# The weight sums of a Strassen–Winograd feed-forward layer in pair order on GpSimd: low products last, stores behind later loads

## The chip, the cores and the metric

The kernel runs on one core of a Trainium2 chip. The metric is the device time of one launch in microseconds; before the change the median of three runs is 1889.56 us (1884.88 to 1890.27).

Five engines work side by side, each with a queue of its own that is served in order: PE (TensorE, matmuls; its loading of weights is listed apart as PEld), DVE (VectorE), ACT (ScalarE), POOL (GpSimd) and SP (SyncE, which issues nearly all DMAs). An instruction that waits holds back everything behind it in its own queue.

## The reference

Two sequences, a prompt of 256 and a sample of 512 positions, go through two layers of a model of width 1024. The first layer mixes positions by an mLSTM in both directions, the second by attention in a window. Behind each mixer stands the feed-forward part, on which the change works:

```python
def conv_ffn(h, w_up, conv_w, conv_b, w_down):          # D_FF = 2816
    u = h @ w_up                                         # 1024 -> 5632
    u = conv_general_dilated(u, conv_w, width 3, one channel each) + conv_b
    g, val = u[..., :D_FF], u[..., D_FF:]
    return (jax.nn.silu(g) * val) @ w_down               # 2816 -> 1024

for l in range(2):
    ...
    x = x + g1 * mixer(rmsnorm(x, norm_g[l, 0]) * (1 + sc1) + sh1)
    h = rmsnorm(x, norm_g[l, 1]) * (1 + sc2) + sh2
    x = x + g2 * conv_ffn(h, ...)
return rmsnorm(x, final_g)
```

All is float32.

## The kernel before

**Precision.** A float32 matrix product is made of three products of rounded halves: high by high, high by low and low by high. `split` makes the halves of a weight tile of 128 x 1024 (`raw`, loaded by SP): ACT casts the high half (`whi`, line 262), then DVE subtracts it from the tile (`wlo`, line 263).

**Up-projection.** The 768 columns of both sequences are halved into two times 384 (H). The 2816 channels are cut into 11 parts (p = 0 to 10), and each part has two units of weights (i = 0 for the gate, 1 for the value). `pair` multiplies one unit by Strassen and Winograd's scheme: seven products of quarters in place of eight. `quarters` is one product: 4 slices of the inner dimension by 3 products of halves, 12 matmuls of 128x128 by 384. A pair has 84 matmuls, a part 168. The products are programmed as B11, T1 (weights `s1h`, `s1l`), T2, B21, T3, B22, T4. I name a pair by part and unit: (3,1) is the second pair of part 3.

The operands of the activations are ready in advance (`yh`, `yl`, `zh`, `zl`). Those of the weights are made on POOL, four instructions a pair on the two loaded tiles `ra` and `rb`: line 1204 (q2 += q3, wants only `rb`), 1207 (into `ra`, wants the split `wa` of `ra` to be done), 1208, and 1216 (into `rb`, wants `s1l` made). From the sums ACT and DVE split `s1`, `wc` and `wb`. `wa` serves B11 and B21, `wc` T2 and B22, `wb` T3 and T4. The tile pool holds five raw tiles, so the loads run about two pairs ahead. ACT also copies sums of PSUM between banks in a pair (lines 1219, 1226, 1232, 1243) and evicts results (1184); DVE adds two of them (1245, 1246).

**Convolution and product.** `conv` makes the three taps (ACT 1489, DVE 1491 and 1492), `silu` the gate (ACT 1499). Then parts 0, 1 and 10 are multiplied by `product` and their down-projection is made part by part. The eight parts 2 to 9 (`g is None`, SOLO = 2, NBLK = 8) go another way: `operands` multiplies gate and value on POOL (line 1510, four instructions a part), `combine` makes Strassen's combinations on DVE (lines 1515 to 1518), and the result is stored to DRAM (`yd`, 1344 KB, line 1520). After the last pair, `blocked` makes the down-projection of the eight parts in seven steps of 96 matmuls. It fetches each step's `yd` (line 1285), loads weights (1289), makes sums on POOL (1300) and stores some of them (`sd`, 1302). The activations `xt` are saved to DRAM in between (`xf`, line 388) and added again at the end.

**Order.** PE, ACT, DVE and POOL get their orders from a scheduler that walks the program with estimated times; `issue_after` binds an instruction behind another. Steps are hung on a pair by dictionaries, `later[p, i]` and `held`, and run in the middle of that pair, behind the fourth copy (`behind`, in `pair`). In before, `operands` of part p hangs on pair (p+1,1), `combine` and the store on (p+2,0). Numbers below are in the order p, i.

## Time and profile before

| | |
|---|---|
| median of 3 runs | 1889.56 us (1884.88 to 1890.27) |
| profiled execution | 1893.23 us, of which the span of instructions 1891.4 us |
| busy: PE, DVE, ACT, POOL | 95%, 72%, 50%, 29% of the span |
| mean granted clock of PE | 0.978 |
| read from and written to HBM | 231.09 MB and 40.38 MB, 144 GB/s over the span |

The pairs of parts 5 to 9 follow each other in a steady pattern: in the first layer from 708.6 to 869.7 us of the span, in the second from about 1524 to 1685 us.

Times in rows are microseconds from the span's start. A row of the timeline has start, duration, engine, line, operation, out<-in and count, then in brackets how long the engine had been idle before and what released it. A row of the waits has the total, the number and the longest. A row of the windows has stretch, length, busy time with instruction counts for each engine, granted clock, share of the DMA engines and GB/s.

### The profile page before, as it was taken

To read this page: it belongs to the slowest core of one execution; us is meant where nothing else is said; L and a number is where in the kernel's file an instruction comes from. 1 tells how busy PE (TensorE), PEld (TensorE's weight loads), DVE (VectorE), ACT (ScalarE), POOL (GpSimd) and SP (SyncE) were. 2 spreads that over 40 slices of the span, in tenths; PEclk is the share of its full clock that TensorE was granted. 3 is DMA by queue.
4 is the path that set the end of the run, shared out by engine and by line. 5 is a ranking of instruction groups with operands and counts; after the bars stand their busy time and mean duration, and the time that the engine had idled before them with its cause. 6 is when DMAs were issued, how large, how long until landed. Compare 5 with 4: busy or idle time off the path is not lost.

```text
span 1891.4 us, 29178 instructions
## 1 busy us (share of the span) xinstructions
PE 1791.8 (95%) x11098; PEld 1674.2 (89%) x11098; DVE 1365.6 (72%) x2093; ACT 952.3 (50%) x1935; POOL 553.0 (29%) x450
## 2 busy tenths in 40 slices
PE   7999999999999989998899999999999999998997
PEld 4988888989998989998899999989989899997997
DVE  4765677885798676776868857767997677777685
ACT  3444434443565455554544556665554555555453
POOL 2101001030124345656220214320242555644201
PEclk9999999999999999999899999999999999998998
DMA  8343566455212433234797321133123232356872
GB/s 328 113 155 125 169 203 228 152 169 189 69 58 66 133 105 117 96 134 169 240 315 239 102 89 45 55 117 111 55 69 123 97 125 97 126 177 195 312 251 67
DMA packets 111735, 273.36 MB, mean 145 GB/s; under 512 B 8599, under 2 KB 51095, under 8 KB 109804
## 3 DMA queue, kind: packets, MB, share of 16 engines
q1 hardware_dynamic: 109292, 263.12, 41.6%
q0 software_dynamic: 2304, 8.39, 1.1%
q8 instruction: 87, 1.43, 0.3%
q14 instruction: 52, 0.43, 0.1%
HBM read 231.09 MB, written 40.38 MB: 144 GB/s over the span
## 4 chain that ended last, share of the span: by engine, by line
PE 55%; DVE 13%; POOL 12%; DMA 9%; issue 7%; ACT 3%; SPq 0%; POOLq 0%; DVEq 0%; ACTq 0%
PE ps L256 24%; PE pa L256 10%; DMA raw<-in_w_dram 7%; POOL slab L1510 4%; DVE wlo L263 4%; PE ps L1174 3%; PE ps L1171 3%; PE ps L1172 3%; POOL raw L1208 2%; PE ps L1343 2%; PE ps L1342 2%; PE ps L1344 2%; POOL raw L1207 2%; POOL raw L1204 2%; PE pa L1010 1%
## 5 line engine op out<-in xcount | busy, mean ns | idle before, releaser
L263 DVE TENSOR_TENSOR wlo<-raw,whi 128x1024 fp32r<-128x1024 f32 x261 | 339.4, 1303 | 103.3 <-ACT whi L262 102.5
L262 ACT CAST whi<-raw 128x1024 fp32r<-128x1024 f32 x261 | 272.8, 1048 | 240.8 <-POOL raw L1208 49.9
L1171 PE MATMUL ps<-zh,whi 128*128 128x384 f32 x504 | 175.6, 348 | 22.3 <-ACT whi L262 13.6
L1174 PE MATMUL ps<-zh,wlo 128*128 128x384 f32 x504 | 175.9, 349 | 21.2 <-DVE wlo L263 21.2
L256 PE MATMUL ps<-zh,whi 128*128 128x256 f32 (+1 forms) x560 | 189.0, 339 | 2.3 <-ACT whi L262 1.7
L256 PE MATMUL ps<-zh,wlo 128*128 128x256 f32 (+1 forms) x560 | 184.5, 331 | 1.5 <-DVE wlo L263 1.5
L256 PE MATMUL ps<-zl,whi 128*128 128x256 f32 (+1 forms) x560 | 185.2, 333 | 0.0
L1172 PE MATMUL ps<-zl,whi 128*128 128x384 f32 x504 | 173.8, 345 | 0.8 <-DVE zl L1128 0.8
L1204 POOL TENSOR_TENSOR raw<-raw 128x512 f32<-128x512 f32 x40 | 64.9, 1623 | 270.2 <-DMA raw<-in_w_dram 246.9
L256 PE MATMUL ps<-slab,whi 128*128 128x384 f32 x512 | 132.3, 340 | 0.9 <-DVE slab L263 0.5
L1491 DVE SCALAR_TENSOR_TENSOR slab<-slab,cstt,slab 128x771 f32<-128x771 f32 x88 | 105.2, 1197 | 36.9 <-ACT slab L1489 36.8
L1171 PEld LDWEIGHTS ps<-zh,whi 128*128 128x128 f32 x504 | 97.6, 194 | 30.2 <-ACT whi L262 14.9
L508 DVE SCALAR_TENSOR_TENSOR ada<-raw,silc,ada 128x1024 f32<-128x1024 f32 x84 | 112.1, 1372 | 14.9 <-DMA raw<-in_adaln_w_dram 14.9
L1174 PEld LDWEIGHTS ps<-zh,wlo 128*128 128x128 f32 x504 | 97.8, 194 | 28.2 <-DVE wlo L263 26.6
L256 PEld LDWEIGHTS ps<-zh,whi 128*128 128x128 f32 x560 | 107.7, 193 | 15.8 <-issue 4.4
L1489 ACT ACTIVATE slab<-slab,cstt 128x772 f32<-128x772 f32 x88 | 91.2, 1036 | 55.8 <-DVE slab L1245 55.3
L256 PEld LDWEIGHTS ps<-zl,whi 128*128 128x128 f32 x560 | 107.5, 193 | 12.0 <-issue 3.4
L256 PEld LDWEIGHTS ps<-zh,wlo 128*128 128x128 f32 x560 | 107.5, 192 | 11.7 <-DVE wlo L263 2.4
L1492 DVE SCALAR_TENSOR_TENSOR slab<-slab,cstt,slab 128x771 f32<-128x771 f32 x88 | 113.8, 1293 | 0.3
L1174 PE MATMUL ps<-yh,wlo 128*128 128x384 f32 x304 | 104.6, 344 | 6.3 <-DVE wlo L263 6.3
L1171 PE MATMUL ps<-yh,whi 128*128 128x384 f32 x304 | 103.7, 341 | 0.0
L1172 PE MATMUL ps<-yl,whi 128*128 128x384 f32 x304 | 103.5, 341 | 0.0
(315 smaller groups left out, 5017.8 us busy)
## 6 DMA issues: line engine op xcount, KB each, us to landing
raw<-in_w_dram SPq DMA_DIRECT2D x248, 512.0 KB, 4.2
raw<-in_adaln_w_dram SPq DMA_DIRECT2D x84, 512.0 KB, 4.7
yd<-slab SPq DMA_DIRECT2D x14, 1344.0 KB, 4.6
slab<-yd SPq DMA_DIRECT2D x14, 768.0 KB, 7.7
sd<-raw POOLq DMA_DIRECT2D x16, 512.0 KB, 5.6
raw<-sd SPq DMA_DIRECT2D x16, 512.0 KB, 5.6
slab<-in_x_dram SPq DMA_DIRECT2D x12, 512.0 KB, 6.5
slab<-in_adaln_w_dram SPq DMA_DIRECT2D x12, 512.0 KB, 10.3
```

The lines of the kernel that those rows point to most:

```text
L256: self.nc.tensor.matmul(out, lhsT, rhs, start=start, stop=stop)
L262: nc.scalar.copy(hi, src)
L263: return nc.vector.tensor_tensor(lo, src, hi.bitcast(F32), ALU.subtract)
L508: stt(acc[:, s], row, w, acc[:, s], ALU.mult, ALU.add)
L1171: mm(o, wh[:, k], hi[k], start=start and k == 0, stop=False, skip_group_check=True)
L1172: mm(o, wh[:, k], lo[k], start=False, stop=False, skip_group_check=True)
L1174: mm(o, wl[:, k], hi[k], start=False, stop=k == 3, skip_group_check=True)
L1204: tt(q[2], q[2], q[3], ALU.add)
L1489: nc.scalar.activation(y, u, AF.Identity, bias=cb, scale=w(1))
L1491: stt(y[:, 1:], u[:, :-1], w(0), y[:, 1:], ALU.mult, ALU.add)
L1492: stt(y[:, :-1], u[:, 1:], w(2), y[:, :-1], ALU.mult, ALU.add)
L1510: nc.gpsimd.tensor_tensor(row[:, p0:p1], yrow[:, 2 + j, b], yrow[:, j, b], ALU.mult)
```

## The change

Line numbers of the kernel after the change are one to three lower in `pair` (1203, 1206, 1207, 1215 for the sums; 1231 for the copy 1232; 1299 and 1301 for 1300 and 1302).

- The first sum of a pair is bound behind the last sum of the pair before it or, where a part's products stand in between, behind these (`summed`).
- `quarters` makes the four low products (`wl` by high) behind the eight others in every product, on one line, 1176.
- The products (line 1510) are put between two pairs: behind the sums of pair (p+1,1), and ahead of the first sum of the next. The combining (now lines 1517 to 1520) comes behind the add into `r1` of that pair (`added`).
- The store of a part (line 1523) comes behind the loads of pair (p+2,1) on SP, and the save of `xf` behind those of pair (4,0).
- The second stream's `yd` is fetched behind the loads of the first step of `blocked`, not ahead of the last pairs, and one stop of `blocked` is dropped.

```diff
@@ quarters
-            if not low:
-                mm(o, wl[:, k], hi[k], start=False, stop=k == 3, skip_group_check=True)
         if low:
             low()
-            for k in range(4):
-                mm(o, wl[:, k], hi[k], start=False, stop=k == 3, skip_group_check=True)
+        for k in range(4):
+            mm(o, wl[:, k], hi[k], start=False, stop=k == 3, skip_group_check=True)
@@ raw / pair
-        self.nc.sync.dma_start(t, src)
+        self.loaded = self.nc.sync.dma_start(t, src)
...
-        tt(q[2], q[2], q[3], ALU.add)
+        with self.tc.issue_after(self.summed.ins) if self.summed else nullcontext():
+            tt(q[2], q[2], q[3], ALU.add)
...
-        tt(q[2], q[3], q[0], ALU.subtract)
+        self.summed = tt(q[2], q[3], q[0], ALU.subtract)
...
-        nc.vector.tensor_tensor(r1[:, col(H) :], b, p5, ALU.add)
+        self.added = nc.vector.tensor_tensor(r1[:, col(H) :], b, p5, ALU.add)
@@ blocked
         fetch(0, (0, 1))
-        fetch(1, (0, 1))
         yield
         fetch(0, (2,))
-        fetch(1, (2,))
-        yield
+        fetch(1)
@@ ffn
+        def store(s, k):
+            nc.sync.dma_start(yd[k // 2 - 1][k % 2] if k > 3 else yd[0][k], s)
+
+        def gather(yrow, k):
+            with self.tc.issue_after(self.summed.ins):
+                s = operands(yrow, k)          # its last product becomes self.summed
+            with self.tc.issue_after(self.added.ins):
+                combine(s)
+            if k == NBLK - 1:
+                self.final = s
+            else:
+                later[SOLO + k + 2, 1] = lambda: store(s, k)
+
+        def put_by():
+            for rng in RANGES:
+                self.save_x(xt, xf, rng)
...
-                        self.pair(pool, u0 + 3 * p + i, bank, rows, p == 1, lambda: [f() for f in then])
+                        self.pair(pool, u0 + 3 * p + i, bank, rows, p == 1, held.pop() if held else None)
+                    if (p, i) in moves:
+                        gather(*moves.pop((p, i)))
+                    if (p, i) in later:
+                        with self.tc.issue_after(self.loaded.ins):
+                            later.pop((p, i))()
...
-                    if p == NPART - 1:
-                        next(tail)
             if g is None:
-                later[p + 1, 1] = lambda: operands(yrow, p - SOLO)
+                moves[p + 1, 1] = yrow, p - SOLO
...
             if p == SOLO:
-                for rng in RANGES:
-                    self.save_x(xt, xf, rng)
+                later[p + 2, 0] = put_by
```

POOL in the steady parts. The tiles 7520 and 7522 before, 7519 and 7521 after, are those of the pair (7,1); 7654 and 7656, then 7658 and 7660, those of (8,0). Before:

```order
L1204 TENSOR_TENSOR raw_7785<-raw_7785 128x512
L1207 TENSOR_TENSOR raw_7522<-raw_7520,raw_7522 128x512
L1208 TENSOR_TENSOR raw_7522<-raw_7522 128x512
L1216 TENSOR_TENSOR raw_7520<-raw_7520,raw_7522 128x512
L1510 TENSOR_TENSOR slab_7586<-slab_7123 128x512
L1510 TENSOR_TENSOR slab_7586<-slab_7123 128x256
L1510 TENSOR_TENSOR slab_7586<-slab_7123 128x512
L1510 TENSOR_TENSOR slab_7586<-slab_7123 128x256
L1204 TENSOR_TENSOR raw_7919<-raw_7919 128x512
L1207 TENSOR_TENSOR raw_7656<-raw_7654,raw_7656 128x512
L1208 TENSOR_TENSOR raw_7656<-raw_7656 128x512
L1216 TENSOR_TENSOR raw_7654<-raw_7654,raw_7656 128x512
```

After:

```order
L1203 TENSOR_TENSOR raw_7519<-raw_7519 128x512
L1206 TENSOR_TENSOR raw_7521<-raw_7519,raw_7521 128x512
L1207 TENSOR_TENSOR raw_7521<-raw_7521 128x512
L1215 TENSOR_TENSOR raw_7519<-raw_7519,raw_7521 128x512
L1510 TENSOR_TENSOR slab_7641<-slab_7127 128x512
L1510 TENSOR_TENSOR slab_7641<-slab_7127 128x256
L1510 TENSOR_TENSOR slab_7641<-slab_7127 128x512
L1510 TENSOR_TENSOR slab_7641<-slab_7127 128x256
L1203 TENSOR_TENSOR raw_7658<-raw_7658 128x512
L1206 TENSOR_TENSOR raw_7660<-raw_7658,raw_7660 128x512
L1207 TENSOR_TENSOR raw_7660<-raw_7660 128x512
L1215 TENSOR_TENSOR raw_7658<-raw_7658,raw_7660 128x512
```

Before, the first sum in a group of four is that of a pair two further on (7785 beside 7520, 7919 beside 7654); after, all four are of one pair, and the products stand between the last sum of one pair and the first of the next.

POOL at the end of the pairs, around the products of part 9; the tiles 8326 and 8328 before, 8320 and 8322 after, are those of the pair (10,1), and 8473 to 8493 are weights of the block phase. Before:

```order
L1300 TENSOR_TENSOR raw_8473<-raw_8473,raw_8475 128x1024
L1302 DMA sd_8183<-raw_8473 128x1024
L1300 TENSOR_TENSOR raw_8491<-raw_8491,raw_8493 128x1024
L1207 TENSOR_TENSOR raw_8328<-raw_8326,raw_8328 128x512
L1302 DMA sd_8183<-raw_8491 128x1024
L1510 TENSOR_TENSOR slab_8392<-slab_7918 128x512
L1510 TENSOR_TENSOR slab_8392<-slab_7918 128x256
L1510 TENSOR_TENSOR slab_8392<-slab_7918 128x512
L1510 TENSOR_TENSOR slab_8392<-slab_7918 128x256
L1208 TENSOR_TENSOR raw_8328<-raw_8328 128x512
L1216 TENSOR_TENSOR raw_8326<-raw_8326,raw_8328 128x512
```

After:

```order
L1203 TENSOR_TENSOR raw_8320<-raw_8320 128x512
L1299 TENSOR_TENSOR raw_8473<-raw_8473,raw_8475 128x1024
L1301 DMA sd_8187<-raw_8473 128x1024
L1206 TENSOR_TENSOR raw_8322<-raw_8320,raw_8322 128x512
L1299 TENSOR_TENSOR raw_8491<-raw_8491,raw_8493 128x1024
L1207 TENSOR_TENSOR raw_8322<-raw_8322 128x512
L1215 TENSOR_TENSOR raw_8320<-raw_8320,raw_8322 128x512
L1510 TENSOR_TENSOR slab_8442<-slab_7922 128x512
L1510 TENSOR_TENSOR slab_8442<-slab_7922 128x256
L1510 TENSOR_TENSOR slab_8442<-slab_7922 128x512
L1510 TENSOR_TENSOR slab_8442<-slab_7922 128x256
L1301 DMA sd_8187<-raw_8491 128x1024
```

The products and the issue of a store have gone from between the second and the third sum of the pair; the second sum of the block phase stands ahead of the third in both.

PE in one product of a pair, as the difference (`whi` and `wlo` are the two halves of its weights; the rows with `pa` behind it are another stage's matmuls):

```order
 L1171 MATMUL ps_4533<-yh,whi_5163 128x384
 L1172 MATMUL ps_4533<-yl,whi_5163 128x384
-L1174 MATMUL ps_4533<-yh,wlo_5164 128x384
 L1171 MATMUL ps_4533<-yh,whi_5163 128x384
 L1172 MATMUL ps_4533<-yl,whi_5163 128x384
-L1174 MATMUL ps_4533<-yh,wlo_5164 128x384
 L1171 MATMUL ps_4533<-yh,whi_5163 128x384
 L1172 MATMUL ps_4533<-yl,whi_5163 128x384
-L1174 MATMUL ps_4533<-yh,wlo_5164 128x384
 L1171 MATMUL ps_4533<-yh,whi_5163 128x384
 L1172 MATMUL ps_4533<-yl,whi_5163 128x384
-L1174 MATMUL ps_4533<-yh,wlo_5164 128x384
```

The third, sixth, ninth and twelfth matmul, which read the low half, leave their places; the four follow in one row behind the twelfth of these rows:

```order
+L1176 MATMUL ps_4533<-yh,wlo_5164 128x384 x4
 L256 MATMUL pa_5217<-inv,nt_4877 128x2
 L256 MATMUL pa_5217<-inv,nt_5128 128x2
```

## The prediction

> **What bounds the kernel now.** I read the page first, for who is busy and who ends the chain.

> ```profile
> PE 1791.8 (95%) x11098; PEld 1674.2 (89%) x11098; DVE 1365.6 (72%) x2093; ACT 952.3 (50%) x1935; POOL 553.0 (29%) x450
> PE 55%; DVE 13%; POOL 12%; DMA 9%; issue 7%; ACT 3%; SPq 0%; POOLq 0%; DVEq 0%; ACTq 0%
> ```

> TensorE is the bound, yet only 55% of the chain that ended last is on it. The groups of matmuls of the pairs, the waits, and a piece of the chain in the middle of a layer tell what takes the rest.

> ```profile
> L1171 PE MATMUL ps<-zh,whi 128*128 128x384 f32 x504 | 175.6, 348 | 22.3 <-ACT whi L262 13.6
> L1174 PE MATMUL ps<-zh,wlo 128*128 128x384 f32 x504 | 175.9, 349 | 21.2 <-DVE wlo L263 21.2
> POOL raw L1204 <- DMA raw<-in_w_dram: 246.9, 31, 24.6
> ACT whi L262 <- POOL raw L1208: 49.9, 26, 7.1
> DVE slab L1515 <- POOL slab L1510: 34.3, 16, 4.9
> 800.17 3.61 DMA raw<-in_w_dram
> 803.92 2.38 POOL raw L1204
> 806.30 1.26 POOL raw L1207
> 807.63 2.09 POOL raw L1208
> 809.75 1.06 ACT whi L262
> ```

> TensorE waits for halves of weights (whi, wlo). They are late because POOL's queue is in order: L1204, which serves a pair further on, waits for that pair's weights, and the current pair's L1207, L1208 and L1216 stand behind it; ScalarE's cast and VectorE's low half come after them. Now the stretches: time of a window, PE busy with its matmuls, then PEld, DVE, ACT, POOL, granted clock, DMA share.

> ```profile
> 708.60:869.70 161.10, 152.36 (x843) 146.31 (x842) 113.57 (x121) 88.79 (x151) 90.56 (x60) 1.00 0.36 123
> 1524.00:1685.00 161.00, 152.38 (x843) 146.32 (x843) 113.53 (x122) 88.61 (x150) 89.20 (x61) 1.00 0.36 124
> 663.90:676.40 12.50, 7.08 (x23) 6.45 (x22) 8.53 (x9) 5.43 (x8) 5.59 (x6) 0.73 0.51 194
> 1478.00:1491.00 13.00, 8.46 (x39) 7.82 (x38) 9.69 (x10) 6.45 (x10) 6.09 (x5) 0.87 0.50 185
> 893.30:912.00 18.70, 8.86 (x28) 7.52 (x27) 9.34 (x8) 5.33 (x8) 10.02 (x10) 0.63 0.41 138
> 1705.00:1724.00 19.00, 10.68 (x38) 9.34 (x37) 10.76 (x9) 5.92 (x9) 11.92 (x10) 0.65 0.44 142
> 742.01 0.34 PE L1171 MATMUL ps<-yh,whi 128*128 128x384 f32 x1
> 747.60 0.34 PE L1174 MATMUL ps<-zh,s1l 128*128 128x384 f32 x1
> ```

> The last two rows are the first and last of 33 matmuls without a gap: 5.59/32 = 0.175 us each. A part is two pairs, 168 matmuls, so 29.4 us unbroken, 2.1 us a quarter of twelve. The first two windows are five parts of each layer, 840 matmuls: 146.7 us unbroken, so 14.4 us are lost in each, 2.9 a part. The four short windows are stalls in which the clock also falls. At 0.175 a matmul they need 3.9 (22), 6.8 (39), 4.7 (27) and 6.6 (38): lost are 8.6, 6.2, 14.0 and 12.4 us, 41.2 in all.

> **The change, part by part.** The sum is made against the profiled execution, 1893.2 us (span 1891.4 and 1.8 around it), which is 3.7 above the median of the runs, 1889.56; that is taken off at the end. A measurement of this kernel can tell about 0.3%, 5.7 us, from no change.

> *POOL pair by pair, and low products last, in the steady parts.* POOL now does a pair's four sums together, and the first waits for no weights of a later pair ahead of the current pair's other three. I walked one part from its first matmul, with the quarters at 2.1 us. The cast of wa comes after the previous pair's B21, and its low half ends some 2.2 us before the pair begins; three sums of 1.3 us then end at about 1.7 us into the pair, cast and low half of wc at about 2.8, and T2, its first user, starts at 6.3. No DMA stands in that chain, and 3.5 us cover it. Low last adds 1.0 us: a quarter asks for wlo at its ninth matmul (8 x 0.175 = 1.4) and not at its third (0.35). The wlo waits in the rows above are mostly of such a size.

> ```profile
> 741.73 0.44 PE L1174 MATMUL ps<-yh,wlo 128*128 128x384 f32 x1 [0.54 <-DVE wlo L263]
> 824.70 5.67 POOL L1510 TENSOR_TENSOR slab<-slab 128x512 f32<-128x512 f32 x4
> 787.08 1.29 POOL L1204 TENSOR_TENSOR raw<-raw 128x512 f32<-128x512 f32 x1 [7.68 <-DMA raw<-in_w_dram]
> 803.91 2.39 POOL L1204 TENSOR_TENSOR raw<-raw 128x512 f32<-128x512 f32 x1 [5.32 <-DMA raw<-in_w_dram]
> 813.41 0.61 ACT L262 CAST s1h<-raw 128x512 fp32r<-128x512 f32 x1
> 814.29 0.49 ACT L1232 COPY ps<-ps 128x384 f32<-128x384 f32 x1
> ```

> What is late next: the products L1510 (5.67) now stand ahead of the next pair's first sum (1.29 to 2.39), so after a part's second pair that sum ends at 8.6 to 10.8; ScalarE's cast s1h waits for it with the copy for T3 (L1231, L1232 before) behind it in its queue, and T3 is due at 10.5. Cast and copy add 1.1, so T3 waits 0 to 1.4; I take 0.45 a part, nearer the lower end because 1.29 is what an undisturbed sum takes. A steady part then takes 29.8: five gain 161.1 - 149.0 = 12.1 a layer, 24.2 in both. Bounds: all 28.8; if T3 waits 1.4 each time, 14.8.

> VectorE's steps, in the timeline:

> ```profile
> 798.93 1.21 DVE L263 TENSOR_TENSOR wlo<-raw,whi 128x1024 fp32r<-128x1024 f32 x1
> 800.07 0.54 DVE L1516 TENSOR_TENSOR slab<-slab 128x384 f32<-128x384 f32 x1
> 800.54 1.01 DVE L1491 SCALAR_TENSOR_TENSOR slab<-slab,cstt,slab 128x771 f32<-128x771 f32 x1
> 801.47 0.68 DVE L263 TENSOR_TENSOR s1l<-raw,s1h 128x512 fp32r<-128x512 f32 x1
> ```

> The combining on VectorE gains a wait, for the last pair's sum into r1, at the start of the next pair. Behind it in VectorE's queue stands wlo for T2, due 7 us later. The products end at about 7.3 us into the pair before, 7 us ahead of it, so L1515's wait for L1510 (34.3 in all) ends. The stores to yd follow the loads of a pair on SP; loads no longer wait behind a store's combining. Both at nothing; that cover gone, the steps ahead of wlo cost 1.1 (two of 0.54) a part.

> *The stall in the pair (3,1).*

> ```profile
> 653.84 1.30 POOL L1207 TENSOR_TENSOR raw<-raw,raw 128x512 f32<-128x512 f32 x1 [16.25 <-DVE wlo L263]
> 657.94 4.66 POOL L1510 TENSOR_TENSOR slab<-slab 128x512 f32<-128x512 f32 x4
> 662.57 1.60 POOL L1208 TENSOR_TENSOR raw<-raw 128x512 f32<-128x512 f32 x1
> ```

> Between L1207 and L1208 stand a later pair's sum and the first products: 8.73 us from start to start, where 1.3 would do. Now the two follow each other at once, about 7.4 us earlier than before, and T2's stall and the fallen clock (0.73 and 0.87 in the windows) go. I take 14.2 of the 14.8 us of both layers; lower bound 0, if the weights themselves are late. The xf stores, now behind (4,0)'s loads on SP, must land before the first products; those now come after all sums of (3,1), and (4,0)'s sums behind them have some 5 us before their user.

> *The stall in (10,1).*

> ```profile
> 888.49 3.08 POOL L1300 TENSOR_TENSOR raw<-raw,raw 128x1024 f32<-128x1024 f32 x1 [3.33 <-DMA raw<-in_w_dram]
> 894.10 3.84 POOL L1510 TENSOR_TENSOR slab<-slab 128x512 f32<-128x512 f32 x4
> 900.28 0.69 PE L1171 MATMUL ps<-zh,whi 128*128 128x384 f32 x1 [6.60 <-ACT whi L262]
> 903.98 0.69 PE L1174 MATMUL ps<-zh,wlo 128*128 128x384 f32 x1 [2.69 <-DVE wlo L263]
> ```

> The products (3.84) and a store's issue leave the way of L1208; the second L1299 (L1300 before), which waits for a DMA, stays ahead of it. The first wait of 6.6 shrinks by about 4.4 to 2.2; the low half has 8 matmuls of cover more, and seven of B21's stand behind T2's high ones. [...] Lower bound: the DMA lands late as now, and only the products' 3.84 and half the rest goes, 10. [...]

> *The block phase, the y fetch and the start.*

> ```profile
> 900.00:940.00 40.00, 35.25 (x176) 33.60 (x177) 33.54 (x43) 22.31 (x36) 10.38 (x7) 0.85 0.70 229
> 980.00:1020.00 40.00, 37.17 (x212) 36.19 (x211) 31.50 (x42) 19.90 (x32) 0.00 (x0) 1.00 0.93 328
> 560.00:600.00 40.00, 36.58 (x198) 33.62 (x198) 38.49 (x36) 22.39 (x36) 21.41 (x10) 1.00 0.24 73
> ```

> The second stream's y (7 x 384 x 4 bytes x 128 = 1.38 MB) moves from 846 us, where the queues had room, behind the block phase's first loads; at 328 GB/s that is 4.2 us. Some of it fits where the share is 0.70; TensorE also arrives there about 10 us earlier. I take 2 us a layer, bounds 0 and 4.2. In part 1 VectorE is 96% busy and POOL's new order puts a sum that waits for s1l ahead of the next pair's: I take 1, bounds -1 and 2. Together 6 in both layers.

> **Sum**: 24.2 + 14.2 + 21.4 - 6 = 53.8; 1893.2 - 53.8 - 3.7 = 1835.7, call it 1836. With every stall gone (28.8 + 41.2) and no cost, 1819.5; some 4.5 us of small waits for halves in the other pairs (the two groups show 34.9 for whi and wlo together, the steady parts and stalls hold most of it) would bring 1815.

> **The rivals.** *A: the steady parts keep their time*, because POOL and VectorE slow each other when packed. For it: 1.29 becomes 2.39. Against it: both are far from full, 90.56 and 113.57 of 161.1. Only the stalls go, 35.6 less 6: 1860; at the worst costs (2 x 6.2) 1866, and with 10 for (10,1) besides, 1878.

> [...]

> A part has 6 wlo, 4 combining steps, 8 convolution steps and 2 s1l on VectorE, 18.9 us, and on POOL 8 sums and the products, 8 x 1.29 + 3.84 = 14.2: 33.1 in series. A part of before takes 161.1/5 = 32.2, so full exclusion does not hold; but it is near enough to leave A a fifth of the chance.

> *B, slower: T3 waits in every part, and the clock falls.* If sums run at 2.39 beside VectorE, the three of wa end at 5.0 into the pair, the products at 10.7, the first sum at 13.1, cast and copy at 14.2: T3, due at 10.5, waits 3.7. That is a part of 33.1 for 32.2, +9 in ten, and the time 1893.2 - 35.6 + 6 + 9 - 3.7 = 1869. It decides when that wait makes the clock fall: half a clock for about 7 us loses some 3.5 more a part, 35 in all: 1904. For it, the order does put the products there; against it, only one or two sums of three in a row are that long (2.38, 1.26, 2.09 in the chain).

> *C: nothing changes*, because the late halves are bound by VectorE, not POOL: 1890. Against it, L1208 holds ScalarE's casts 26 times, 49.9 us in all, up to 7.1.

> **How the numbers follow.** The forecast 0.63, A 0.22, B 0.09, C 0.03; 0.03 lies between C and A or just above C. Faster: forecast, A, and 0.01 of the rest, 0.86; same 0.03; slower 0.11, B and the last 0.02. The range reaches from 1815, with every stall gone, to 1872, past A with its costs and some of its worse case.

> **What would show it.** Right: in the steady windows 165 matmuls or more in 31 us; no L1203 waiting for a DMA ahead of an L1206; clock 1.00 at 664 to 680 and at the end of the pairs. A shows as parts of 32 with the waits of TensorE moved to other halves; B as a wait of L1171 for ScalarE's L1231 each part and a clock under 1. The forecast is wrong if the DMA waits of the block phase grow by more than 10 us a layer.

## The result and the profile after

The change moved the time by nothing that can be measured: 1888.72 us in the median of 12 runs (1886.57 to 1894.56) against 1887.14 of before on the same chip, ratio 1.0011 with an interval of 0.9996 to 1.0025. I had forecast 1836. The profiled execution has a span of 1890.1 us, 1891.4 before.

The page and the groups of matmuls of the pairs show what the change did reach, and what took its place:

```profile
PE 1788.5 (95%) x11098; PEld 1678.4 (89%) x11098; DVE 1404.9 (74%) x2093; ACT 952.4 (50%) x1935; POOL 575.9 (30%) x450
L1171 PE MATMUL ps<-zh,whi 128*128 128x384 f32 x504 | 177.3, 352 | 41.2 <-ACT ps L1231 24.8
L1176 PE MATMUL ps<-zh,wlo 128*128 128x384 f32 x504 | 112.7, 345 | 0.0
```

The waits of the same kernel (total, times, longest):

```profile
POOL raw L1203 <- DMA raw<-in_w_dram: 49.4, 2, 24.8
ACT s1h L262 <- POOL raw L1203: 62.3, 18, 4.8
```

TensorE's waits for wlo, 21.2 us in this group before, are gone, and POOL's first sum waits for weights twice and not 31 times. In their place ScalarE's cast s1h waits 62.3 us for L1203, and L1171 waits 24.8 us for L1231, the copy for T3: the wait named under rival B.

To see where in the program time went or came from, I take the starts of ScalarE's copy behind B11 (L1219 before, L1218 after), once in each pair. In both lists: pair (3,1), (4,0) and (10,0) of the first layer, (1,0), (3,1), (4,0) and (10,0) of the second. Before:

```profile
657.93 0.46 ACT L1219 COPY ps<-ps 128x384 f32<-128x384 f32 x1 [1.64 <-PE ps L1174]
683.09 0.47 ACT L1219 COPY ps<-ps 128x384 f32<-128x384 f32 x1
874.99 0.50 ACT L1219 COPY ps<-ps 128x384 f32<-128x384 f32 x1
1365.85 0.47 ACT L1219 COPY ps<-slab 128x384 f32<-128x384 f32 x1
1474.10 0.46 ACT L1219 COPY ps<-ps 128x384 f32<-128x384 f32 x1 [1.64 <-PE ps L1174]
1497.05 0.47 ACT L1219 COPY ps<-ps 128x384 f32<-128x384 f32 x1
1688.71 0.50 ACT L1219 COPY ps<-ps 128x384 f32<-128x384 f32 x1
```

After:

```profile
662.11 0.46 ACT L1218 COPY ps<-ps 128x384 f32<-128x384 f32 x1
680.75 0.50 ACT L1218 COPY ps<-ps 128x384 f32<-128x384 f32 x1
874.80 0.50 ACT L1218 COPY ps<-ps 128x384 f32<-128x384 f32 x1
1363.72 0.48 ACT L1218 COPY ps<-slab 128x384 f32<-128x384 f32 x1
1474.34 0.46 ACT L1218 COPY ps<-ps 128x384 f32<-128x384 f32 x1
1492.97 0.50 ACT L1218 COPY ps<-ps 128x384 f32<-128x384 f32 x1
1686.99 0.50 ACT L1218 COPY ps<-ps 128x384 f32<-128x384 f32 x1
```

With the same copy of (1,0) in the first layer (551.15 and 551.67), that for T3 in the pairs (10,1) (907.58 and 1719.78 before, 900.33 and 1712.84 after) and the spans, the differences of the stretches are:

| stretch | first layer | second layer | both | forecast |
|---|---|---|---|---|
| parts 1 to 3, up to (3,1) | +3.7 | +2.4 | +6.0 | +2 |
| stall of (3,1) | -6.5 | -4.3 | -10.8 | -14.2 |
| steady parts, (4,0) to (10,0) | +2.1 | +2.4 | +4.5 | -24.2 |
| (10,0) and (10,1) | -7.1 | -5.2 | -12.3 | -21.4 |
| block phase and what follows | +5.1 | +5.6 | +10.8 | +4 |

With 0.5 us more ahead of (1,0) in the first layer, these rows make up the 1.3 us by which the two spans differ: gains of 23.1 us at the two stalls against 21.8 lost elsewhere. They come from one profiled execution of each kernel.

The steady parts are the large miss. In one of them, after: POOL's last sum of the pair, the products and the next pair's first sum, then ScalarE's cast and the copy behind it, and T3's first matmul. The last row is T3's first matmul in the next part.

```profile
789.62 1.30 POOL L1215 TENSOR_TENSOR raw<-raw,raw 128x512 f32<-128x512 f32 x1
790.88 7.37 POOL L1510 TENSOR_TENSOR slab<-slab 128x512 f32<-128x512 f32 x4
798.21 2.00 POOL L1203 TENSOR_TENSOR raw<-raw 128x512 f32<-128x512 f32 x1
800.24 0.62 ACT L262 CAST s1h<-raw 128x512 fp32r<-128x512 f32 x1 [3.56 <-POOL raw L1203]
800.77 0.47 ACT L1231 COPY ps<-ps 128x384 f32<-128x384 f32 x1
801.29 0.45 PE L1171 MATMUL ps<-zh,whi 128*128 128x384 f32 x1 [1.33 <-ACT ps L1231]
833.27 0.45 PE L1171 MATMUL ps<-zh,whi 128*128 128x384 f32 x1 [2.22 <-ACT ps L1231]
```

A window behind the second of these waits; its last three columns are the granted clock, the DMA share and GB/s:

```profile
834.00:836.50 2.50, 2.50 (x10) 2.50 (x9) 1.72 (x2) 2.09 (x4) 0.19 (x1) 0.50 0.01 3
```

The pair's first matmul began at 789.28. The sums ended at 1.6 us into it, as forecast (1.7). The products then took 7.37 and not 5.67, the sum 2.00, cast and copy 1.1: T3, due at 10.5, began at 12.0. In the next part the sums end only at 2.6 us, T3 begins at 12.9, after a wait of 2.22, and behind that wait the granted clock is 0.50. So it goes in turn, one part at full clock and one that has half the clock for some 3.4 us.

### The profile page after: what moved, and what is told of

It is laid out like the page before. It is cut to its first block, busy times and chain, and to the rows that moved or that the text cites. A ratio compares the mean times of both kernels' runs of the same rounds, so it can differ in the third digit from the quotient of the medians.

```text
span 1890.1 us, 29143 instructions
## 1 busy us (share of the span) xinstructions
PE 1788.5 (95%) x11098; PEld 1678.4 (89%) x11098; DVE 1404.9 (74%) x2093; ACT 952.4 (50%) x1935; POOL 575.9 (30%) x450
## 5 line engine op out<-in xcount | busy, mean ns | idle before, releaser
L263 DVE TENSOR_TENSOR wlo<-raw,whi 128x1024 fp32r<-128x1024 f32 x261 | 365.1, 1401 | 102.6 <-ACT whi L262 97.0
L262 ACT CAST whi<-raw 128x1024 fp32r<-128x1024 f32 x261 | 272.8, 1048 | 203.6 <-POOL raw L1207 67.5
L1171 PE MATMUL ps<-zh,whi 128*128 128x384 f32 x504 | 177.3, 352 | 41.2 <-ACT ps L1231 24.8
L1206 POOL TENSOR_TENSOR raw<-raw,raw 128x512 f32<-128x512 f32 x40 | 52.8, 1320 | 303.6 <-issue 254.5
L1171 PEld LDWEIGHTS ps<-zh,whi 128*128 128x128 f32 x504 | 98.6, 196 | 47.5 <-ACT ps L1231 29.3
L1490 DVE SCALAR_TENSOR_TENSOR slab<-slab,cstt,slab 128x771 f32<-128x771 f32 x88 | 119.1, 1355 | 4.7 <-ACT slab L1488 4.6
L1510 POOL TENSOR_TENSOR slab<-slab 128x512 f32<-128x512 f32 x64 | 117.8, 1871 | 0.0
L256 PEld LDWEIGHTS ps<-zh,wlo 128*128 128x128 f32 x560 | 106.5, 191 | 12.1 <-DVE wlo L263 2.9
L1176 PE MATMUL ps<-zh,wlo 128*128 128x384 f32 x504 | 112.7, 345 | 0.0
L1491 DVE SCALAR_TENSOR_TENSOR slab<-slab,cstt,slab 128x771 f32<-128x771 f32 x88 | 110.7, 1258 | 1.3
L262 ACT CAST nt<-slab 128x384 fp32r<-128x384 f32 x112 | 57.2, 513 | 104.6 <-PE ps L1340 46.6
L1171 PE MATMUL ps<-yh,whi 128*128 128x384 f32 x304 | 103.4, 340 | 0.0
L256 PE MATMUL pa<-slab,whi 128*128 128x256 f32 (+1 forms) x448 | 100.2, 318 | 2.8 <-DVE slab L592 2.8
```

What stands on the lines that cost most here:

```text
L256: self.nc.tensor.matmul(out, lhsT, rhs, start=start, stop=stop)
L262: nc.scalar.copy(hi, src)
L263: return nc.vector.tensor_tensor(lo, src, hi.bitcast(F32), ALU.subtract)
L1171: mm(o, wh[:, k], hi[k], start=start and k == 0, stop=False, skip_group_check=True)
L1176: mm(o, wl[:, k], hi[k], start=False, stop=k == 3, skip_group_check=True)
L1206: tt(q[0], q[2], q[0], ALU.subtract)
```

## The experiments

Each time is a median beside runs of the kernel before on the same chip; the ratio has its interval. The steady part is the distance from the copy of (5,0) to that of (10,0) in the profile of each, divided by five. The experiments ran on several chips, on which the medians of the kernel before differ by up to 3 us, so that differences in us between two rows are good to about that.

| kernel | us | ratio to before | steady part, both layers |
|---|---|---|---|
| before | 1887 to 1890 | 1 | 31.84, 31.85 |
| after | 1888.72 | 1.0011 (0.9996 to 1.0025) | 32.04, 32.04 |
| copy ahead | 1876.7 | 0.9935 (0.9917 to 0.9953) | 31.58, 31.52 |
| sum ahead | 1871.41 | 0.9903 (0.9883 to 0.9924) | 30.70, 30.65 |
| fetch back | 1878.32 | 0.9944 (0.9927 to 0.9961) | 32.03, 32.03 |
| part 1 unbound | 1884.49 | 0.9976 (0.9960 to 0.9991) | 32.22, 32.04 |
| before, low last | 1878.91 | 0.9949 (0.9935 to 0.9963) | 31.57, 32.29 |
| after, low mixed | 1906.2 | 1.0089 (1.0075 to 1.0104) | 32.95, 33.01 |
| three edits | 1853.53 | 0.9808 (0.9791 to 0.9825) | 30.66, 30.64 |
| three edits, silu moved | 1847.57 | 0.9778 (0.9762 to 0.9794) | 30.27, 30.27 |
| before, pair order | 1877.35 | 0.9928 (0.9901 to 0.9955) | 30.61, 30.60 |
| after, stores back | 1892.87 | 1.0016 (0.9998 to 1.0033) | 32.22, 32.02 |
| three edits, silu moved, block sums bound | 1845.89 | 0.9768 (0.9743 to 0.9793) | 30.26, 30.28 |
| before, pair order and low last, part 1 unbound | 1855.37 | 0.9835 (0.9812 to 0.9859) | 30.73, 30.73 |

**The copy ahead of the cast.** My theory was that T3 waits because ScalarE's queue holds its copy behind a cast that waits for POOL. The rival was that POOL and VectorE, packed against each other, are the floor.

```diff
-        self.fp_copy_split(s1h, s1l, q[2])
+        with self.tc.issue_after(self.forked.ins) if self.forked else nullcontext():
+            self.fp_copy_split(s1h, s1l, q[2])
...
-        fork = nc.scalar.copy(d, b)
+        self.forked = fork = nc.scalar.copy(d, b)
```

> The kernel after, with ScalarE's cast s1h of the next pair bound behind the copy L1231 of the current one. Theory Q (ScalarE's queue: the copy for T3 stands behind a cast that waits for POOL's products and sum): the waits of L1171 for L1231, 24.8 us in the profile of after, and the fallen clock behind them, some 8 us, go; about 1860 us, with steady parts near 29.8. Theory P (VectorE and POOL packed against each other are the floor): the waits move to other halves, steady parts stay at 32, 1884 to 1890. It also moves a sum of the block phase behind the last products at the end of the pairs, worth up to 4 us a layer either way.

It is 0.65% faster than before, less than half of what my theory asked. The wait for that copy is gone, but the same two groups show others:

```profile
L1171 PE MATMUL ps<-zh,whi 128*128 128x384 f32 x504 | 172.4, 342 | 12.1 <-ACT ps L1219 9.4 <-ACT nt L1243 2.7
L1176 PE MATMUL ps<-zh,wlo 128*128 128x384 f32 x504 | 109.6, 338 | 15.1 <-DVE wlo L263 15.1
```

A steady part gains only 0.5 on the kernel after: with products and sum as late as before, VectorE's wlo is late next, 15.1 us in all. So ScalarE's queue is where T3 waited, but taking that away alone brings little; that the lateness comes from POOL, the next run shows.

**The sum ahead of the products.** Here the other end of the chain is moved: the products come after the next pair's first sum.

```diff
-            tt(q[2], q[2], q[3], ALU.add)
+            first = tt(q[2], q[2], q[3], ALU.add)
+        if between:            # the products and combining of the part, in pair (p+2,0)
+            self.summed = first
+            between()
```

> The kernel after, with the next pair's first sum on POOL ahead of the products, not behind them. Theory Q: L1203 ends by 4 us into the pair, the copy for T3 is in time though ScalarE's order is as before; about 1860 us, steady parts near 29.8. Theory P: products of 7.4 us beside VectorE stay the floor, 1884 to 1890; or the sum waits for its weights as it did in the kernel before, and a part keeps 32.

It is 0.97% faster than before and a steady part takes 30.7. ScalarE's order of cast and copy is as in after, and the copy for T3 (L1234) now waits for TensorE, so what made T3 late was the products ahead of the sum. The products still take 7.12 there; their length is no floor. One wait a part is left, which the timeline places behind a silu in ScalarE's queue:

```profile
787.46 7.12 POOL L1513 TENSOR_TENSOR slab<-slab 128x512 f32<-128x512 f32 x4
790.24 0.46 ACT L1234 COPY ps<-ps 128x384 f32<-128x384 f32 x1 [0.61 <-PE ps L1176]
796.16 0.85 ACT L1501 ACTIVATE slab<-slab 128x772 f32<-128x772 f32 x1 [3.45 <-DVE slab L1494]
796.91 0.52 ACT L1182 COPY slab<-ps 128x128 f32<-128x128 f32 x2
797.48 0.44 PE L1171 MATMUL ps<-yh,whi 128*128 128x384 f32 x1 [0.96 <-ACT slab L1182]
```

**The fetch of y back.**

```diff
         fetch(0, (0, 1))
+        fetch(1, (0, 1))
         yield
         fetch(0, (2,))
-        fetch(1)
+        fetch(1, (2,))
```

> The kernel after, with the second stream's fetch of y back ahead of the last pairs. Theory F (the moved 1.38 MB is what the block phase pays, about 5 us a layer): 1879 us, waits of the block phase as in the kernel before. Theory D (the block phase is bound by its DMAs, whoever arrives earlier waits): 1887 to 1890, no change.

1878.32 against 1879 expected by theory F: the moved fetch is worth 10.4 us of the time after, 5.2 a layer, about all that the block phase lost. In after, the window from 900 to 1000 us, and the fetch on SP's queue:

```profile
900.00:1000.00 100.00, 91.24 (x510) 87.70 (x509) 81.15 (x99) 51.02 (x83) 27.50 (x17) 1.00 0.87 302
```

```profile
915.29 1.88 SPq L1284 DMA_DIRECT2D slab<-yd  x3
```

With the fetch back, the same two:

```profile
900.00:1000.00 100.00, 96.09 (x534) 92.70 (x534) 84.52 (x105) 52.40 (x86) 29.92 (x18) 0.99 0.88 298
```

```profile
850.33 4.86 SPq L1284 DMA_DIRECT2D slab<-yd  x4
```

The DMA engines are as busy, 0.87 and 0.88, but 24 matmuls more lie in the 100 us. With these shares, and 0.93 from 980 to 1020 us in the kernel before, the phase is near its DMA bound, and 1.38 MB there cost 5.2 us a layer, no less than the 4.6 that they take at 302 GB/s.

**Part 1 unbound.**

```diff
+                    if p == 1:
+                        self.summed = None
```

> The kernel after, with the sums of part 1 unbound, so that the second pair's sums come ahead of the first pair's last one, as before. If that order costs what the trace shows (a wait of 4.4 us at 565 us and the fallen clock, 4 us in the first layer, 2.4 in the second): 1882 to 1883 us. If the delay there is absorbed by the parts that follow: 1888.

1884.49, 4.2 us under after; 1882 to 1883 was expected. The two intervals, 0.9960 to 0.9991 here and 0.9996 to 1.0025 for after, are barely apart. The first layer's wait, in after, was this:

```profile
565.51 2.24 POOL L1203 TENSOR_TENSOR raw<-raw 128x512 f32<-128x512 f32 x1
566.56 2.02 DVE L1491 SCALAR_TENSOR_TENSOR slab<-slab,cstt,slab 128x771 f32<-128x771 f32 x1
568.61 0.85 ACT L1498 ACTIVATE slab<-slab 128x772 f32<-128x772 f32 x1 [4.80 <-DVE slab L1491]
569.87 0.69 PE L1171 MATMUL ps<-zh,whi 128*128 128x384 f32 x1 [4.27 <-ACT nt L1242]
```

POOL's later sums fall beside VectorE's convolution, a silu waits for that, and a copy of ScalarE stands behind the silu. In this kernel the way from the copy of (1,0) to that of (3,1) is 3.4 us shorter than in after in the first layer and 3.5 in the second.

**Low products last, alone and taken away.** The edit of `quarters` (the first piece of the change's diff) alone on the kernel before, and the kernel after with that piece taken back:

> The kernel before with one edit: the four low products last in every quarter. Theory L (the slack of 1.0 us alone does what was hoped of the steady parts): of 27.5 us that TensorE waited there for wlo nearly all that is in gaps of 0.5 to 1.0 goes, about 15 us, 1873; the two stalls with a fallen clock stay. Theory W (the chain POOL, cast, low half is late as a whole, and the next instruction waits instead): under 5 us, 1884 or more.

> The kernel after with the low products mixed in again. Theory L: the halves of the pair's first sums are late by 0.5 to 1 us again, 1895 to 1900. Theory W: the pair order alone has brought wlo in time and T3's wait for the copy stays what it is, 1887 to 1891.

Alone it gains 0.51%, and 1878.91 us lies between the two forecasts. The gain is not a shorter steady part (31.57 and 32.29): there theory W is right. The groups say why:

```profile
L1171 PE MATMUL ps<-zh,whi 128*128 128x384 f32 x504 | 174.7, 347 | 35.5 <-ACT ps L1217 16.7
L1176 PE MATMUL ps<-zh,wlo 128*128 128x384 f32 x504 | 110.8, 340 | 5.4 <-DVE wlo L263 5.0
```

The waits for wlo fall from 21.2 to 5.0, and those of L1171 rise from 22.3 to 35.5; what is gained lies at (3,1), where the copies of this kernel show 6.0 and 3.9 us less from (3,1) to (4,0). Without it the kernel after is 17.5 us slower by the medians (15 beside the kernel before on each chip), beyond both forecasts. Neither theory's mechanism shows: wlo is waited for only 2.5 us (L), while T3 waits not the same (W) but longer, 1.35 to 2.63 us in a part's one pair and 0.38 in the other, and 37.4 us in all where after has 24.8. Why that wait grows isn't settled.

**Three edits together, and the silu moved.** The three diffs above (the sum ahead, the fetch back, part 1 unbound); then also

```diff
+                    if held and i == 1 and p >= SOLO:
+                        with self.tc.issue_after(self.evicted.ins):   # last copy of evict(r1, a)
+                            held.pop()()
```

> Three edits together on the kernel after: the next pair's first sum ahead of the products, the fetch of y back, the sums of part 1 unbound. If the three causes are separate places, their gains add: 1888.7 - 17.3 - 10.4 - 4.2 = 1857 us. If what is won ahead of the block phase is waited for there (its DMAs as the floor), 1865 to 1870.

> As the three together, and ScalarE's silu behind the eviction of the pair that follows and not ahead of it. In the run with the sum ahead, each steady part had one wait left, 0.96 us and 1.1 lost, of T3 for an eviction that stands behind a silu; without it a part takes 29.5 us, ten parts give 11 us, 1846. If another copy takes its place in ScalarE's queue (silu now stands ahead of the copy of u3): 1853 to 1858.

1853.53 where the sum of the three gains gave 1857, so the three causes lie in separate places and what is won ahead of the block phase is kept. The silu gives 6 us more by the medians, 1847.57, with a steady part of 30.3: just over half of the 11 that I had put on it. The intervals of the two kernels still touch.

**Pair order alone, and both first edits on before.** The binding `summed` is put into the kernel before, and the products are left inside the pair. POOL then has them behind the next first sum by the scheduler's own choice. The second kernel adds the edit of `quarters` and leaves part 1 unbound.

```diff
+        with self.tc.issue_after(self.summed.ins) if self.summed else nullcontext():
-        tt(q[2], q[2], q[3], ALU.add)
+            tt(q[2], q[2], q[3], ALU.add)
...
-        tt(q[2], q[3], q[0], ALU.subtract)
+        self.summed = tt(q[2], q[3], q[0], ALU.subtract)
```

> The kernel before with one edit: the first sum of a pair bound behind the last one of the pair before; the products stay inside the pair, and so stand behind the next first sum. If T3's wait of the kernel after comes only from products ahead of that sum, this order is free of it: the stall of (3,1) goes (14 us in both layers), the steady parts keep small wlo waits without the low products last, that of (10,1) stays, part 1 loses 4 and 2.4: 1870 to 1880 us. If pair order itself makes T3 late: 1888 or more, with waits of L1171 for the copy of T3 above 1 us.

> Only the two first edits of the change, on the kernel before: pair order on POOL from part 2 on, and low products last everywhere; products, stores and fetches stay where they were, and the first sum comes ahead of the products by itself. If products, stores and fetch brought nothing but loss: as the run of three edits or better, 1845 to 1855. If the products between the pairs are worth something at (3,1) and (10,1) that this order lacks: 1860 to 1870.

With pair order alone the time is 1877.35, as expected, and a steady part takes 30.6, a gain of 1.2 a part that the whole change did not have; the sum, the products and the copy for T3 (L1233), which again waits for TensorE, in the timeline:

```profile
787.99 2.00 POOL L1205 TENSOR_TENSOR raw<-raw 128x512 f32<-128x512 f32 x1
789.95 6.64 POOL L1512 TENSOR_TENSOR slab<-slab 128x512 f32<-128x512 f32 x4
794.34 0.46 ACT L1233 COPY ps<-ps 128x384 f32<-128x384 f32 x1 [0.67 <-PE ps L1174]
801.31 0.44 PE L1171 MATMUL ps<-zh,whi 128*128 128x384 f32 x1 [0.33 <-ACT nt L1244]
```

The two edits together, with nothing else moved and part 1 unbound, give 1855.37, within 2 us of the three edits on the kernel after. Moving the products and the stores as well thus brought 2 us at most, less than the chips differ by. Low last adds nothing to a steady part there (30.73), but with part 1 unbound the time falls by 22 us elsewhere: in the profiles 14 of it lie in (10,0) and (10,1), and 8 in parts 1 to 3.

**Stores back.**

```diff
-                later[SOLO + k + 2, 1] = lambda: store(s, k)
+                store(s, k)
...
-                later[p + 2, 0] = put_by
+                put_by()
```

> The kernel after with the stores of yd and the save of xf back where they were. The prediction cost both moves at nothing: 1888.7 within 3 us. If the later stores are what crowds the loads in the steady parts, it is faster by 5 us or more; if the earlier ones did, slower.

1892.87, 4.2 us above after where 3 was allowed, but with a ratio of 1.0016 to before where after has 1.0011: no difference that these intervals can tell. The yd stores hardly moved on SP by this edit, the save of xf did. So costing the save of xf at nothing was right; for the yd stores this run shows little.

**The block phase's first sums bound behind (10,1).**

```diff
-                        op(r, r, raw(b(k)), how)
+                        with self.tc.issue_after(self.ended.ins) if i == 0 else nullcontext():
+                            op(r, r, raw(b(k)), how)
```

> As the run with the silu moved, and the first sums of the block phase bound behind the last sum of the pair (10,1). There T2 still waited 4.3 us for a cast behind a POOL sum that waits for a DMA, and the clock fell. If that sum is the cause, about 8 us a layer go: 1832. If the raw tiles that it holds longer make the block phase's loads late, part comes back as waits there: 1840 to 1848.

1845.89, ratio 0.9768 beside 0.9778 without it: not told apart. T2's wait of 4.34 us in (10,1) went and the way from the copy of (10,0) to that for T3 in (10,1) became 8.6 us shorter in the first layer and 8.3 in the second; what follows took it back, with a wait in the last product of (10,1) and one in the block phase (L1346):

```profile
883.92 0.45 PE L1171 MATMUL ps<-zh,whi 128*128 128x384 f32 x1 [1.61 <-ACT nt L1246]
889.28 0.44 PE L1346 MATMUL pa<-nt,whi 128*128 128x384 f32 x1 [2.83 <-DVE nt L263]
```

The copy of (1,0) in the next layer was 1.3 us later than without the edit. That the block phase wants early the same sum that holds up the pairs is how I read it; no run takes the two apart.

## Why the prediction was wrong

**Bound and diagnosis** were right. POOL's order held the weights' halves late: pair order alone brings a steady part from 31.8 to 30.6, and POOL's first sum no longer waits for weights there.

**The steady parts**, forecast 29.8 and measured 32.04, are the step that failed. I had named what is late next, the sum behind the products and the copy for T3 behind its cast, and walked it to the right places (sums ending at 1.7, measured 1.6 and, in every second part, 2.6; T3 due at 10.5). But I put 0.45 us on it, nearer the lower end, with two durations that were not those of the new place. The products took 7.37 where I used 5.67 from a place with less VectorE work beside it, and the sum 2.00 where I leaned to 1.29. With these the walk gives 1.6 + 7.4 + 2.0 + 1.1 = 12.1, which is what happened. My upper end of 10.8 for that sum does not follow from its rows either: 1.7 + 5.67 + 2.39 is 9.8, which leaves T3 a wait of 0.4 at most and not 1.4. I had also left the clock out of the forecast: T3 is late by 1.5 and 2.4 us in turn, which costs 2 us a part, and behind the second kind, in every second part, the granted clock was 0.50 for 3.41 us.

**Rival B** was the mechanism, at a smaller size: T3 waited 1.31 to 2.58 us and not 3.7, and the three sums ahead of the products were not slow (1.29 to 1.30); it was the products and the sum behind them. I gave it 0.09. **Rival A** named the price, parts of 32, and part of the cause: POOL and VectorE do slow each other. The four products of a part take 3.84 us where VectorE is busy for 0.65 us of that time (at 894.10 in the kernel before), 5.67 where it is for 3.78 (at 824.70 there), and 7.37 where it is for 7.31 (at 790.88 in the kernel after). But that is no floor for a part: with the sum ahead of the products the same work fits in 30.7 and 30.3 us. Full exclusion, POOL and VectorE never at work at the same time, would put 33.1 us of undisturbed durations in series, an estimate from VectorE's 1.21, 0.54, 1.01 and 0.68 and POOL's 1.29 and 3.84, so it does not hold in a part of 30.3. In the 7.37 us VectorE did what undisturbed takes about 4.8, an estimate from 1.21 for wlo and 1.01 for a convolution step; with 3.84 for the products that is 8.6 of work in 7.4 us, so only a little of it overlapped.

**The stall of (3,1)** went, for 10.8 us and not 14.2. **(10,1)** gained 12.3 and not 21.4. The 21.4 is the 26.4 lost there less 2.5 us of waiting a layer, and no run shows that 2.5 us of waiting cost only themselves: in the kernel before, the granted clock was 0.50 from 1799.29 to 1802.68, with a wait of 2.12 us up to 1799.47, and stayed at 1.00 behind one of 2.02 us up to 987.25. In the kernel after the wait left over was not 2.2 but 3.78 us, for the DMA behind L1299 that I had seen, and the clock still fell (0.65 over the window below). POOL's L1207 stands behind L1299, ScalarE's cast waits for L1207, and the copy that T2 needs stands behind the cast (timeline of after, then a window):

```profile
889.10 2.88 POOL L1299 TENSOR_TENSOR raw<-raw,raw 128x1024 f32<-128x1024 f32 x1 [2.16 <-DMA raw<-in_w_dram]
891.95 1.25 POOL L1207 TENSOR_TENSOR raw<-raw 128x512 f32<-128x512 f32 x1
893.24 1.04 ACT L262 CAST whi<-raw 128x1024 fp32r<-128x1024 f32 x1 [5.61 <-POOL raw L1207]
894.61 0.49 ACT L1218 COPY ps<-ps 128x384 f32<-128x384 f32 x1
895.15 0.55 PE L1171 MATMUL ps<-zh,whi 128*128 128x384 f32 x1 [3.78 <-ACT ps L1218]
```

```profile
894.00:898.40 4.40, 3.25 (x11) 3.25 (x12) 3.53 (x3) 3.36 (x7) 4.40 (x4) 0.65 0.59 189
```

**The block phase** cost 10.8 for 4: I took 2 us a layer, less than half of the fetch, as time lost, and the run with the fetch back shows all of it, 5.2 a layer, more than my upper bound of 4.2. **Part 1** cost 6.0 for 2, again through an engine's queue one step further on than I had looked.

So every term was off in one direction, and the gains that did come were cancelled by three separate costs, each shown by a run that undoes it: 14 us in the ten steady parts (32.0 against 30.7 with the sum ahead), 10 in the block phase, 4 in part 1.

## What to carry to other kernels

When an instruction is moved to be early, ask what it now stands ahead of on its own queue, and then what stands behind the waiting one on the next queue; a lateness of one or two microseconds there, here T3's 1.5 and 2.4, comes back in every part. Price a moved instruction by its duration beside the engines that work at its new place, not at its old one: here 7.4 us for 5.7. A change of several edits is worth taking apart, since the two that helped, with part 1 left unbound, give 1855 us alone and the others cancelled them, and the best of these kernels, 1846 to 1848 us, keeps the sum ahead of the products.

## What the runs showed of the hardware

```profile
830.49:833.88 3.39, 1.17 (x7) 0.85 (x6) 1.59 (x3) 1.66 (x3) 1.69 (x1) 1.00 0.55 155
833.91:837.30 3.39, 3.39 (x12) 3.39 (x12) 1.81 (x2) 2.45 (x6) 0.99 (x1) 0.50 0.01 2
```

In the kernel with part 1 unbound a longer wait, 2.58 us up to 699.66, did not bring the clock down. Counted back from that kernel's next fall, at 732.75, it lies across two steps:

```profile
695.20:698.60 3.40, 1.88 (x11) 1.55 (x9) 2.26 (x2) 0.00 (x0) 3.38 (x2) 1.00 0.35 105
698.62:702.01 3.39, 2.35 (x13) 2.35 (x14) 2.28 (x3) 3.39 (x6) 0.00 (x0) 1.00 0.15 56
```

TensorE was idle for 2.2 us of the step ahead of the fall, and for 1.5 and 1.0 of these two. By this estimate the clock would have stayed up or not, with the 2.5 us of waiting that I had left in (10,1), by where in the steps they fell.
